# A two-layer mixer network in one program: every engine's order written out by hand, normalisation done in place

## Chip, core and metric

The kernel runs on one core of a Trainium2 chip. The metric is the device time of one execution in microseconds (us), the median of several runs. One more execution is taken by the hardware profiler; its times are those of the trace.

## What is computed

The input `x` is 256 rows of 1024 numbers; a vector `c` sets scale, shift and gate of each step (the modulation). Two layers follow, each a mixer and a feed-forward, with a layer norm after each of the four residual sums, then a hybrid mixer and a gated convolution. Cut to what matters:

```python
for i in range(DEPTH):                       # 2
    sh1, sc1, g1, sh2, sc2, g2 = split(silu(c) @ w_ada[i] + b_ada[i], 6)
    u = x * (1.0 + sc1) + sh1
    y = gla_mixer(u) if i == 0 else chunk_attention(u)
    x = layer_norm(ALPHA * x + (1 + g1) * y, ln_g, ln_b)
    u = x * (1.0 + sc2) + sh2
    y = square(relu(u @ w1)) @ w2            # 1024 -> 4096 -> 1024
    x = layer_norm(ALPHA * x + (1 + g2) * y, ln_g, ln_b)
x = x + hybrid_mixer(rms_norm(x))            # pooled, attention over chosen keys, gates
x = x + conv_ffn(rms_norm(x))
out = rms_norm(x)
```

All in float32. The GLA mixer is a gated linear attention in chunks of 64 rows, whose gate goes through a projection of 16 columns.

## The kernel before, in words

**Products.** A float32 product is made of three products in a shorter format (`mm3`, L264 to L268): each operand is a high part and a rest, and high x high, rest x high, high x rest are summed in PSUM. The weights come in chunks of at most 128x1024, in one list `CHUNKS` for the whole program. `load` (L247) fetches a chunk into a `raw` tile (four of these), ScalarE copies the high part (`hi`, L257), VectorE subtracts the rest (`lo`, L262). Near a phase's end the subtraction is made in two halves. Eight `hi`/`lo` pairs are held, and at times two more in the mixer's tiles `qk` and `v`. The same four `raw` tiles carry the weights of the modulation: `ada_gen` (L279) sums them on VectorE, L298 for the gates (into `acc`) and L300 for scale and shift.

**Rows.** The 256 rows are two halves `h` of 128. The mixers are a generator for each half, and `run` (L1273) lets half 0 go ahead by one chunk, at a phase's start and end by eight (`LEAD`), so that one half multiplies while the other is normalised. The feed-forwards take both halves together, with the last eight tiles half by half (`tail`).

**Startup** (L1168) makes scale and shift of the first step and multiplies the first 16 chunks (keys and values of the GLA mixer) into six PSUM banks: for each half two of the four `y` banks and one of the two `ps` banks. `gla_phase` empties them on ScalarE (L601 to L603) and then uses `ps` again for the projection to the first queries and the gate's 16 columns (`lr`, 272 wide); `lr` is copied by VectorE (L607), and `gla_core` transposes it and goes on.

**Layer norm.** `resid_ln` and `ln_chain`: VectorE adds gate times `y` to `x` into `z`, in two halves, with row statistics (L403 to L407); GpSimd makes rstd and shift in three steps (L410 to L412); ScalarE normalises both halves of `z` (L415); TensorE transposes `z` (L373), and `make_u` applies scale and shift and splits into `uh` and `ul`, the operands of the next phase. Gain and bias of the norm go into `x` afterwards (L393, L394).

**Order.** The startup is emitted in program order (`manual_schedule`). For all the rest a scheduler sorts the instructions of every engine: by the place where they were emitted, moved up by the offsets of `high_priority` blocks (`HPL`, `HPB`, `HPE`, ...), and by when it expects the operands. Each engine then runs its list in order; SyncE's list is that of the transfers.

Of the kernel before, what the change touches and what calls it, by code (L numbers as in the profile page):

```python
# [15 lines left out]
LN_EPS = 1e-5  # L16
# [7 lines left out]
HPL = 20  # L24
HPB = 234
HPE = 194
NACT = 5
XLOW = 40
FP = 88
W0 = 2  # L30
W1 = 8
HPC = 50
HPG = 0
# [5 lines left out]
F1 = 8  # L39
YL = 2  # L40
# [145 lines left out]
class K:  # L186
    def __init__(self, nc, tc, dr, out, dbg=None):
        self.nc, self.tc, self.dr, self.out, self.dbg = nc, tc, dr, out, dbg or {}
        self.loaded = 0
        self.ch = {}  # L190
        self.apos = self.bpos = 0
        self.uid = 0

    def nm(self, s):
        self.uid += 1
        return f"{s}_{self.uid}"

# [49 lines left out]
    def load(self):  # L247
# [22 lines left out]
    def split(self, src, n):  # L270

        xh = self.sb(512, f"hh{self.h}", 2, F32R)
        xl = self.sb(512, f"hl{self.h}", 2, F32R)
# [5 lines left out]
    def ada_gen(self):  # L279
# [3 lines left out]
        for idx, (layer, v) in enumerate(ADA):  # L283
# [23 lines left out]
            if gate:  # L307
# [3 lines left out]
                self.gate_rows(*late)  # L311
# [5 lines left out]
            yield  # L317

# [30 lines left out]
    def make_u(self, h, srcs, S, O):  # L349
        nc = self.nc  # L350
        uh, ul = (t[:, h * 1024:h * 1024 + 1024] for t in self.U)
        for j, src in enumerate(srcs):
            t = self.t2().rearrange("p (k t) -> p k t", t=128)
            sl = slice(j * 512, j * 512 + 512)
            if O is None and j == 1:
                nc.vector.tensor_tensor(t, src, S[:, j * 4:j * 4 + 4, None].to_broadcast([128, 4, 128]), op=ALU.mult)
            else:
                for k in range(4):
                    kk = j * 4 + k
                    if kk < NACT:  # L360
                        nc.scalar.activation(t[:, k, :], src[:, k, :], AF.Identity, scale=S[:, kk:kk + 1], bias=0.0 if O is None else O[:, kk:kk + 1])
                    else:
                        nc.vector.tensor_scalar(t[:, k, :], src[:, k, :], S[:, kk:kk + 1], O[:, kk:kk + 1], op0=ALU.mult, op1=ALU.add)
            t = t.rearrange("p k t -> p (k t)")
            nc.scalar.activation(uh[:, sl], t, AF.Copy)
            nc.vector.tensor_sub(ul[:, sl], t, uh[:, sl].bitcast(F32))
# [17 lines left out]
    def resid_ln(self, h, y, i, S, O):  # L384

        nc = self.nc
        x = self.x[h]
        with self.tc.high_priority(offset=HPL if h == 0 else HPB):
            pre = self.ln_chain(h, y, S, O)
        with self.tc.high_priority(offset=-XLOW):  # L390
            for j in range(2):
                sl = slice(j * 512, j * 512 + 512)
                nc.vector.tensor_mul(x[:, sl], pre[:, sl], self.lng[:, sl])  # L393
                nc.vector.tensor_add(x[:, sl], x[:, sl], self.lnb[:, sl])  # L394

    def ln_chain(self, h, y, S, O):
        nc = self.nc
        x = self.x[h]
        pre = self.sb(1024, "z")
        st = self.sb(12, "st", 2)  # L400
        for j in range(2):
            sl = slice(j * 512, j * 512 + 512)
            nc.vector.tensor_mul(pre[:, sl], y[j], self.Guse[:, sl])  # L403
            nc.vector.scalar_tensor_tensor(pre[:, sl], x[:, sl], ALPHA, pre[:, sl], op0=ALU.mult, op1=ALU.add)
            nc.vector.bn_stats(st[:, j * 6:j * 6 + 6], pre[:, sl])
# [7 lines left out]
        for j in range(2):  # L413
            sl = slice(j * 512, j * 512 + 512)
# [20 lines left out]
    def use(self, h):  # L435
        i = self.pos[h]
        self.pos[h] += 1
        if self.bg[h] is not None and next(self.bg[h], 0) == 0:
            self.bg[h] = None
# [122 lines left out]
    def ff_phase(self, after):  # L562
        nc = self.nc

        def squared(p):
            r = self.t2()
            with self.tc.high_priority(offset=HPE):
                nc.scalar.activation(r, p, AF.Relu)
            nc.scalar.activation(r, r, AF.Square)
            return r  # L570

        def head(h, tiles):
            for g in range(FFH // 4):
                yield from self.proj(h)
                self.h = h
                t = self.transposed(squared(self.res))
                self.keep_tiles(tiles, g * 4, self.split(t.rearrange("p k t -> p (k t)"), 512), 4, h)
                yield

        box = []  # L580

        def column(i, tiles):
# [4 lines left out]
            if i % 2 == 1:  # L587
                self.h = i // 2 % 2
                self.keep_tiles(tiles, i - 1, self.split(squared(p), 512), 2)
# [4 lines left out]
    def gla_phase(self, h, after):  # L594
# [17 lines left out]
        nc.scalar.activation(q[:, 256:], self.res, AF.Copy, scale=qs)  # L612
        yield
        pair = []
        for j in range(2):
            sl = slice(j * 512, j * 512 + 512)
            yield from self.proj(h)
            if j == 0:
                self.drain(h)
# [773 lines left out]
```

## Time and profile before

| | |
|---|---|
| median of 3 runs | 1071.26 us (1071.01 to 1071.87) |
| profiled execution | 1077.91 us |
| its span in the trace | 1076.1 us |
| granted TensorE clock, mean over the span | 0.987 |
| busy share of TensorE, VectorE, ScalarE, GpSimd | 95, 71, 53, 5% |
| moved by the transfers | 228.98 MB, 213 GB/s over the span |

The profiled execution is one of its own and 6.6 us above the median; every row of the trace belongs to it. TensorE's busy time is that of pipelined products, whose start to start time is shorter than one's duration. Granted clock is the share of full speed: 1.00 is 2.4 GHz, 0.50 is 1.2 GHz. "Idle before" of a row names what the engine waited for last.

### The profile page before, as it was taken

What the parts mean: (1) busy time and instruction counts of PE and PEld (TensorE: products, weight loads), DVE (VectorE), ACT (ScalarE), POOL (GpSimd) and SP (SyncE); (2) the same over time, 40 slices, a digit from 0 to 9 for tenths busy, and PEclk for the clock granted to TensorE, in tenths of its full rate; (3) what the DMA queues carried; (4) which work ended last, traced back from release to release, by engine and by line L of the source; (5) the groups of instructions that cost most, each with busy time, mean ns of one, the idle gap of its engine ahead of it and who ended that gap; (6) DMA issues with size and microseconds to landing.
All of it is one profiled execution on the core that took longest, in us unless ns stands there. A gap on an engine that the chain in (4) does not pass through costs nothing.

```text
span 1076.1 us, 15174 instructions
## 1 busy us (share of the span) xinstructions
PE 1025.8 (95%) x5628; PEld 856.0 (80%) x5628; DVE 759.3 (71%) x1162; ACT 572.8 (53%) x875; POOL 49.6 (5%) x93
## 2 busy tenths in 40 slices
PE   7999979999998999998999999899999999999997
PEld 4777757998986758686899888676878778999996
DVE  6879886777777776758666543788444678877764
ACT  4654456445555454535755553565555368655543
POOL 0000220000000000001000000200000001000000
PEclk9999999999999998999999999999999999999999
DMA  9998957888885685933877754344345655655521
GB/s 343 334 315 293 314 171 240 299 293 299 299 293 169 208 297 190 297 124 124 301 244 234 233 175 149 117 132 143 113 140 192 201 165 165 220 192 178 189 86 40
DMA packets 69478, 228.98 MB, mean 213 GB/s; under 512 B 7430, under 2 KB 12806, under 8 KB 69404
## 3 DMA queue, kind: packets, MB, share of 16 engines
q1 hardware_dynamic: 69404, 228.01, 62.9%
q8 instruction: 44, 0.72, 0.3%
q14 instruction: 30, 0.25, 0.1%
HBM read 226.93 MB, written 1.05 MB: 212 GB/s over the span
## 4 chain that ended last, share of the span: by engine, by line
PE 53%; DMA 13%; DVE 8%; ACT 6%; issue 3%; POOL 2%; POOLq 0%; ACTq 0%; SPq 0%; DVEq 0%
PE ps L266 10%; DMA raw<-in_w_dram 10%; PE ps L268 10%; PE ps L267 10%; PE y L266 6%; PE y L268 6%; PE y L267 6%; DMA raw<-in_ada_dram 3%; DVE lo L262 3%; ACT hi L257 3%; PE y L782 1%; PE pc L373 1%; PE y L756 1%; PE y L373 1%; DVE raw L300 1%
## 5 line engine op out<-in xcount | busy, mean ns | idle before, releaser
L262 DVE TENSOR_TENSOR lo<-raw,hi 128x1024 fp32r<-128x1024 f32 (+3 forms) x290 | 306.6, 1070 | 132.2 <-ACT hi L257 129.5
L257 ACT ACTIVATE hi<-raw 128x1024 fp32r<-128x1024 f32 (+2 forms) x250 | 262.5, 1055 | 256.1 <-DMA raw<-in_w_dram 84.1
L266 PE MATMUL ps<-hi,uh 128*128 128x512 f32 (+3 forms) x408 | 161.7, 396 | 2.1 <-ACT t L886 0.9
L267 PE MATMUL ps<-lo,uh 128*128 128x512 f32 (+3 forms) x408 | 159.1, 390 | 1.1 <-DVE lo L1260 1.1
L268 PE MATMUL ps<-hi,ul 128*128 128x512 f32 (+3 forms) x408 | 158.7, 389 | 0.0
L266 PE MATMUL y<-hi,hh 128*128 128x512 f32 x378 | 152.5, 403 | 3.7 <-ACT hh L274 3.7
L267 PE MATMUL ps<-ul,hi 128*128 128x256 f32 x536 | 151.3, 282 | 0.0
L268 PE MATMUL y<-hi,hl 128*128 128x512 f32 x378 | 151.0, 401 | 0.1
L266 PE MATMUL ps<-uh,hi 128*128 128x256 f32 x536 | 151.0, 282 | 0.0
L267 PE MATMUL y<-lo,hh 128*128 128x512 f32 x378 | 151.0, 399 | 0.0
L268 PE MATMUL ps<-uh,lo 128*128 128x256 f32 x536 | 150.8, 281 | 0.0
L266 PEld LDWEIGHTS ps<-uh,hi 128*128 128x128 f32 x536 | 100.8, 188 | 2.4
L267 PEld LDWEIGHTS ps<-ul,hi 128*128 128x128 f32 x536 | 100.5, 188 | 2.4
L268 PEld LDWEIGHTS ps<-uh,lo 128*128 128x128 f32 x536 | 101.3, 189 | 0.0
L266 PEld LDWEIGHTS ps<-hi,uh 128*128 128x128 f32 x408 | 78.2, 192 | 18.9 <-ACT t L886 1.6
L267 PEld LDWEIGHTS ps<-lo,uh 128*128 128x128 f32 x408 | 78.2, 192 | 17.3 <-DVE lo L1260 3.0
L268 PEld LDWEIGHTS ps<-hi,ul 128*128 128x128 f32 x408 | 77.9, 191 | 15.6 <-issue 1.6
L266 PEld LDWEIGHTS y<-hi,hh 128*128 128x128 f32 x378 | 71.9, 190 | 19.7 <-ACT hh L274 4.8
L268 PEld LDWEIGHTS y<-hi,hl 128*128 128x128 f32 x378 | 71.6, 190 | 18.2 <-DVE hl L275 1.5
L267 PEld LDWEIGHTS y<-lo,hh 128*128 128x128 f32 x378 | 71.8, 190 | 15.0 <-issue 0.7
L257 ACT ACTIVATE qk<-raw 128x1024 fp32r<-128x1024 f32 x42 | 44.5, 1061 | 50.5 <-DMA raw<-in_w_dram 20.7
L262 DVE TENSOR_TENSOR v<-raw,qk 128x1024 fp32r<-128x1024 f32 (+1 forms) x49 | 52.2, 1072 | 26.9 <-ACT qk L257 26.5
(290 smaller groups left out, 1526.0 us busy)
## 6 DMA issues: line engine op xcount, KB each, us to landing
raw<-in_w_dram SPq DMA_DIRECT2D x302, 512.0 KB, 4.3
raw<-in_ada_dram SPq DMA_DIRECT2D x80, 512.0 KB, 4.6
br<-in_rows_dram SPq DMA_DIRECT2D x12, 256.0 KB, 5.1
bias<-in_relb_dram SPq DMA_DIRECT2D x12, 256.0 KB, 5.8
lng<-in_rows_dram SPq DMA_DIRECT2D x5, 512.0 KB, 3.8
raw<-in_w_dram SPq DMA_DIRECT2D x8, 256.0 KB, 6.2
lnb<-in_rows_dram SPq DMA_DIRECT2D x4, 512.0 KB, 6.2
z<-in_ada_dram SPq DMA_DIRECT2D x3, 512.0 KB, 7.0
```

Of the source, the lines that this page charges most:

```text
L257: self.nc.scalar.activation(hi, raw, AF.Copy)
L262: self.nc.vector.tensor_sub(lo[:, sl], raw[:, sl], hi[:, sl].bitcast(F32))
L266: mm(out, xh, wh, start=start, stop=False)
L267: mm(out, xh, wl, start=False, stop=False)
L268: mm(out, xl, wh, start=False, stop=stop)
L300: nc.vector.scalar_tensor_tensor(raw, raw, 1.0, self.crow, op0=ALU.mult, op1=ALU.mult, accum_out=t[:, k:k + 1])
L373: self.nc.tensor.transpose(p[:, k * 128:k * 128 + 128], src[:, k * 128:k * 128 + 128], self.ident)
L756: nc.tensor.matmul(p[:, i * N:i * N + N], qT[r0:r0 + 64, hd // 2, :], kT[r0:r0 + 64, hd // 2, :N], start=True, stop=True)
L782: nc.tensor.matmul(o[:, hd * 64:hd * 64 + 64], pT[:, (i * nkb + kb) * 128:(i * nkb + kb) * 128 + 128], v[:, kb, hd * 64:hd * 64 + 64], sta ...
```

## The change

The scheduler is left out of the whole program: `run` is emitted under `manual_schedule`, so the order of emission is each engine's order. What should not stand at once behind its predecessor becomes a task. `mm3` counts time (0.000457 us per column for each of its three products at `self.clock`), and a task says with `yield` how much of that must be emitted before it goes on; `tick` runs the tasks that are due. Transposes, the GLA core, the attention cores and the last part of each normalisation are such tasks. The normalisation is done in place in `x` (ScalarE the first half, VectorE the second), and GpSimd keeps only the power. The halved subtraction is gone. The order of the transfers stays nearly the same.

```diff
     def mm3(self, out, xh, xl, wh, wl, start, stop):
...
+        self.clock += 3 * 0.000457 * out.free_size()
+        self.tick()
...
+    def spawn(self, gen):
+        task = [self.clock, gen]
+        self.tasks.append(task)
+        self.advance(task)
+        return task
+
+    def advance(self, task):
+        d = next(task[1], None)
...
+            task[0] = self.clock + d
+
+    def tick(self):
...
+        for task in list(self.tasks):
+            if task[1] is not None and task[0] <= self.clock:
+                self.advance(task)
...
-        n = raw.shape[1]
-        near = any(e - W0 <= self.loaded < e + W1 for e in ENDS[:-1])
-        for a in ((0, n // 2), (n // 2, n)) if near else ((0, n),):
-            sl = slice(*a)
-            self.nc.vector.tensor_sub(lo[:, sl], raw[:, sl], hi[:, sl].bitcast(F32))
+        self.nc.vector.tensor_sub(lo, raw, hi.bitcast(F32))
...
-            nc.vector.scalar_tensor_tensor(pre[:, sl], x[:, sl], ALPHA, pre[:, sl], op0=ALU.mult, op1=ALU.add)
-            nc.vector.bn_stats(st[:, j * 6:j * 6 + 6], pre[:, sl])
+            nc.vector.scalar_tensor_tensor(x[:, sl], x[:, sl], ALPHA, z[:, sl], op0=ALU.mult, op1=ALU.add)
+            nc.vector.bn_stats(st[:, j * 6:j * 6 + 6], x[:, sl])
         mv = self.sb(2, "mv", 2)
         nc.vector.bn_aggr(mv, st)
         v = self.sb(8, "rv", 4)
-        g = nc.gpsimd
-        g.tensor_scalar(v[:, 0:1], mv[:, 1:2], LN_EPS, None, op0=ALU.add)
-        g.tensor_tensor(v[:, 1:2], v[:, 0:1], self.mhalf[:, 0:1], op=ALU.pow)
-        g.tensor_scalar(v[:, 2:3], mv[:, 0:1], -1.0, v[:, 1:2], op0=ALU.mult, op1=ALU.mult)
-        for j in range(2):
-            sl = slice(j * 512, j * 512 + 512)
-            nc.scalar.activation(pre[:, sl], pre[:, sl], AF.Identity, scale=v[:, 1:2], bias=v[:, 2:3])
-        self.make_u(h, [self.transposed(pre[:, j * 512:j * 512 + 512]) for j in range(2)], S, O)
-        return pre
+        nc.vector.tensor_scalar(v[:, 0:1], mv[:, 1:2], LN_EPS, None, op0=ALU.add)
+        nc.gpsimd.tensor_tensor(v[:, 1:2], v[:, 0:1], self.mhalf[:, 0:1], op=ALU.pow)
+        nc.vector.tensor_scalar(v[:, 2:3], mv[:, 0:1], v[:, 1:2], -1.0, op0=ALU.mult, op1=ALU.mult)
+        nc.scalar.activation(x[:, sls[0]], x[:, sls[0]], AF.Identity, scale=v[:, 1:2], bias=v[:, 2:3])
+        nc.vector.tensor_scalar(x[:, sls[1]], x[:, sls[1]], v[:, 1:2], v[:, 2:3], op0=ALU.mult, op1=ALU.add)
+        yield 5.6
+        self.make_u(h, [self.transposed(x[:, sl]) for sl in sls], S, O)
+        if nxt is not None:
+            yield 12.0 if h == 0 else 8.0
+        for sl in sls:
+            nc.vector.tensor_mul(x[:, sl], x[:, sl], self.lng[:, sl])
+            nc.vector.tensor_add(x[:, sl], x[:, sl], self.lnb[:, sl])
...
-        nc.scalar.activation(q[:, :256], self.res[:, :256], AF.Copy, scale=qs)
         lr = self.sb(16, "lr", 2)
         nc.vector.tensor_copy(lr, self.res[:, 256:272])
+        nc.scalar.activation(q[:, :256], self.res[:, :256], AF.Copy, scale=qs)
         box = {}
-        self.bg[h] = self.gla_core(h, lr, q, k, v, box)
+        core = self.spawn(self.gla_core(h, lr, q, k, v, box))
...
     def gla_core(self, h, lr, q, k, v, box):

         nc = self.nc
+        yield 1.4
+        while h == 1 and "z" not in self.gla:
+            yield 0.7
         p = self.pc()
         nc.tensor.transpose(p[0:16, :128], lr, self.ident)
...
-        with self.tc.manual_schedule():
-            self.startup()
+        self.startup()
...
-            k.run()
+            with tc.manual_schedule():
+                k.run()
```

**ScalarE at the start of the GLA mixer.** `hi` are high parts of chunks 16 to 23, `v0`, `qk0`, `v1`, `qk1` the emptied startup banks; `ps_19` and `ps_22` are the two `ps` banks. Before:

```order
L257 ACTIVATE hi_104_458<-raw_103_456 128x816
L602 ACTIVATE qk0_131_536<-y_17_86 128x512
L257 ACTIVATE hi_107_464<-raw_106_462 128x816
L601 ACTIVATE v0_132_537<-ps_19_88 128x512
L603 ACTIVATE v0_132_537<-y_18_87 128x512
L602 ACTIVATE qk1_134_551<-y_20_89 128x512
L257 ACTIVATE hi_110_470<-raw_109_468 128x544
L601 ACTIVATE v1_135_552<-ps_22_91 128x512
```

And now (the five rows ahead of these are the `hi` of chunks 16 to 20):

```order
L279 ACTIVATE hi_120_509<-raw_119_507 128x1024
L279 ACTIVATE hi_123_515<-raw_122_513 128x1024
L279 ACTIVATE hi_126_521<-raw_125_519 128x1024
L631 ACTIVATE v0_132_536<-ps_19_88 128x512
L632 ACTIVATE qk0_131_535<-y_17_86 128x512
L633 ACTIVATE v0_132_536<-y_18_87 128x512
L631 ACTIVATE v1_135_551<-ps_22_91 128x512
L279 ACTIVATE hi_138_567<-raw_137_565 128x1024
```

The six copies moved behind all eight loads, and the first of them is the one from `ps_19`, whose bank the 272-wide projection `ps_133` uses next.

**VectorE at the same place.** `lo` are rests of chunks, `acc` the sum for the first gate over eight `raw` tiles, `lr` the gate's 16 columns. Before:

```order
L262 TENSOR_TENSOR lo_118_505<-raw_116_502,hi_117_504 128x1024
L607 COPY lr_151_625<-ps_133_541 128x16
L262 TENSOR_TENSOR lo_121_511<-raw_119_508,hi_120_510 128x1024
L607 COPY lr_152_634<-ps_136_556 128x16
L646 COPY glT_159_648<-pc_158_646 16x128
L262 TENSOR_TENSOR lo_124_517<-raw_122_514,hi_123_516 128x1024
```

And now:

```order
L280 TENSOR_TENSOR lo_127_522<-raw_125_519,hi_126_521 128x1024
L318 SCALAR_TENSOR_TENSOR acc_128_525<-raw_129_529,cact_14_83,acc_128_525 128x1024
...
L280 TENSOR_TENSOR lo_139_568<-raw_137_565,hi_138_567 128x1024
...
L280 TENSOR_TENSOR lo_145_601<-raw_143_598,hi_144_600 128x1024
L318 SCALAR_TENSOR_TENSOR acc_128_525<-raw_148_608,cact_14_83,acc_128_525 128x1024
L318 SCALAR_TENSOR_TENSOR acc_128_525<-raw_149_611,cact_14_83,acc_128_525 128x1024
L318 SCALAR_TENSOR_TENSOR acc_128_525<-raw_150_614,cact_14_83,acc_128_525 128x1024
L636 COPY lr_151_623<-ps_133_540 128x16
L636 COPY lr_152_632<-ps_136_555 128x16
```

The copy of `lr` stood behind `lo_118`; now three more `lo` (`lo_121`, `lo_124`, `lo_127`), two later ones and all eight sums stand ahead of it.

**ScalarE at the end of the first feed-forward.** `t2_618` is the last activation, `hh1_619` its high part. Before:

```order
L257 ACTIVATE hi_616_2952<-raw_615_2950 128x1024
L257 ACTIVATE hi_622_2990<-raw_621_2988 128x1024
L257 ACTIVATE qk1_625_3003<-raw_624_3001 128x1024
L257 ACTIVATE hi_628_3016<-raw_627_3014 128x1024
L568 ACTIVATE t2_618_2981<-ps_611_2906 128x512
L569 ACTIVATE t2_618_2981<-t2_618_2981 128x512
L274 ACTIVATE hh1_619_2984<-t2_618_2981 128x512
```

And now:

```order
L279 ACTIVATE hi_616_2943<-raw_615_2941 128x1024
L588 ACTIVATE t2_618_2971<-ps_611_2898 128x512
L589 ACTIVATE t2_618_2971<-t2_618_2971 128x512
L294 ACTIVATE hh1_619_2974<-t2_618_2971 128x512
L279 ACTIVATE hi_622_2980<-raw_621_2978 128x1024
L279 ACTIVATE qk1_625_2992<-raw_624_2990 128x1024
```

The activation moved ahead of three loads.

## Rows read from the trace of the kernel before

**Rows 1.** The page, busy us of each engine (share of the span):
```profile
PE 1025.8 (95%) x5628; PEld 856.0 (80%) x5628; DVE 759.3 (71%) x1162; ACT 572.8 (53%) x875; POOL 49.6 (5%) x93
```
**Rows 2.** Waits of TensorE: total us, times, longest
```profile
PE pc L373 <- ACT z L415: 17.8, 8, 4.1
...
PE y L266 <- ACT hh L274: 3.7, 1, 3.7
PE y L373 <- ACT cs L762: 2.6, 2, 1.8
...
PE pc L373 <- ACT t L569: 2.0, 2, 1.7
```
**Rows 3.** Windows: stretch, length, busy us by engine, granted clock, DMA share, GB/s
```profile
13.00:45.00 32.00, 31.12 (x127) 23.76 (x127) 30.24 (x60) 16.16 (x32) 0.99 (x2) 1.00 1.02 395
58.30:143.50 85.20, 78.85 (x382) 59.75 (x381) 75.75 (x119) 41.31 (x66) 12.31 (x14) 1.00 0.89 297
...
135.00:150.00 15.00, 11.22 (x46) 8.13 (x46) 10.92 (x25) 10.23 (x16) 4.68 (x5) 0.89 0.57 182
...
400.00:415.00 15.00, 15.00 (x67) 11.22 (x67) 8.61 (x13) 7.82 (x16) 0.20 (x1) 0.67 0.70 209
```
**Rows 4.** Timeline, third norm (after the first feed-forward): start, us, engine, line [idle before]
```profile
334.78 0.69 DVE L403 TENSOR_TENSOR z<-y,G 128x512 f32<-128x512 f32 x1 [1.15 <-PE y L268]
...
337.31 0.68 DVE L262 TENSOR_TENSOR lo<-raw,hi 128x512 fp32r<-128x512 f32 x1
...
337.90 0.20 DVE L407 BATCH_NORM_AGGREGATE mv<-st 128x2 f32<-128x12 f32 x1
...
338.20 0.55 POOL L410 TENSOR_SCALAR rv<-mv 128x1 f32<-128x1 f32 x1 [93.14 <-DVE mv L407]
...
338.83 0.99 POOL L411 TENSOR_TENSOR rv<-rv,mhalf 128x1 f32<-128x1 f32 x1
...
340.22 1.52 ACT L415 ACTIVATE z<-z,rv 128x512 f32<-128x512 f32 x2 [1.56 <-POOL rv L412]
...
341.09 0.44 PE L373 MATMUL pc<-const,z 128*128 128x128 f32 x2 [1.43 <-ACT z L415]
```
**Rows 5.** Timeline of VectorE at the start of the GLA mixer
```profile
58.06 0.17 DVE L607 COPY lr<-ps 128x16 f32<-128x16 f32 x1
...
62.45 1.20 DVE L262 TENSOR_TENSOR lo<-raw,hi 128x1024 fp32r<-128x1024 f32 x1
...
83.01 1.28 DVE L298 SCALAR_TENSOR_TENSOR acc<-raw,cact,acc 128x1024 f32<-128x1024 f32 x1
```
**Rows 6.** Timeline of TensorE at the same place
```profile
51.94 0.40 PE L268 MATMUL ps<-hi,ul 128*128 128x512 f32 x1
...
52.17 0.29 PE L266 MATMUL ps<-hi,uh 128*128 128x272 f32 x1
...
58.29 0.28 PE L643 MATMUL pc<-const,lr 128*16 128x128 f32 x1
```
**Rows 7.** Timeline of ScalarE and TensorE at the first feed-forward's end
```profile
321.07 1.06 ACT L257 ACTIVATE hi<-raw 128x1024 fp32r<-128x1024 f32 x1 [0.17 <-DMA raw<-in_w_dram]
...
326.98 1.06 ACT L257 ACTIVATE hi<-raw 128x1024 fp32r<-128x1024 f32 x1 [0.86 <-DMA raw<-in_w_dram]
...
327.95 0.58 ACT L568 ACTIVATE t<-ps 128x512 f32<-128x512 f32 x1
...
329.90 0.50 PE L266 MATMUL y<-hi,hh 128*128 128x512 f32 x1 [3.65 <-ACT hh L274]
```
**Rows 8.** Timeline of ScalarE at the start of the GLA mixer
```profile
50.26 0.60 ACT L601 ACTIVATE v<-ps 128x512 f32<-128x512 f32 x1
...
61.01 1.06 ACT L257 ACTIVATE hi<-raw 128x1024 fp32r<-128x1024 f32 x1 [0.81 <-DMA raw<-in_w_dram]
```
**Rows 9.** Timeline of VectorE in the attention
```profile
381.42 0.69 DVE L819 TENSOR_TENSOR cs<-y,bias 128x512 f32<-128x512 f32 x1
...
390.95 1.23 DVE L300 SCALAR_TENSOR_TENSOR raw<-raw,crow 128x1024 f32<-128x1024 f32 x1
```

More of the change, by code (lines that the diff above doesn't have):

```diff
@@ L39 @@
 F1 = 8
+NS = 8
 YL = 2
@@ L317, in ada_gen, with gate_last @@
             yield
+    def gate_last(self, *late):
+        yield 4.0
+        self.gate_rows(*late)
     def gate_rows(self, layer, v, acc):
@@ L566, in squared, with turn @@
             r = self.t2()
-            with self.tc.high_priority(offset=HPE):
-                nc.scalar.activation(r, p, AF.Relu)
+            nc.scalar.activation(r, p, AF.Relu)
             nc.scalar.activation(r, r, AF.Square)
             return r
+        def turn(h, g, tiles):
+            r = squared(self.res)
+            yield 2.4
+            t = self.transposed(r)
+            self.keep_tiles(tiles, g * 4, self.split(h, t.rearrange("p k t -> p (k t)"), 512), 4, h)
         def head(h, tiles):
@@ L587, in column @@
             if i % 2 == 1:
-                self.h = i // 2 % 2
-                self.keep_tiles(tiles, i - 1, self.split(squared(p), 512), 2)
+                self.spawn(kept(i, p, tiles))
             yield
@@ L612, in gla_phase, with gated @@
         nc.scalar.activation(q[:, 256:], self.res, AF.Copy, scale=qs)
+        box["q"] = True
         yield
         pair = []
+        tasks = []
+        def gated(j, sl, before):
+            while "o" not in box:
+                yield 0.7
+            self.finish(before)
+            if j == 0:
+                box["on"] = self.sb(1024, f"v{h}")
+                self.taken.add(h)
+            o, r, on = box["o"], box["r"], box["on"]
+            for d in range(2 * j, 2 * j + 2):
+                ds = slice(d * 256, d * 256 + 256)
+                nc.vector.scalar_tensor_tensor(on[:, ds], o[j][:, ds.start - j * 512:ds.stop - j * 512], r[:, d:d + 1], g2[:, ds], op0=ALU.mult, op1=ALU.mult)
+            yield 2.8
+            t = self.transposed(on[:, sl])
+            if j == 1:
+                self.taken.discard(h)
+            pair.append(self.split(h, t.rearrange("p k t -> p (k t)"), 512))
         for j in range(2):
@@ L742, in banks, with core @@
         return [[par + 2 * (b * nb + i) for i in range(nb)] for b in range(4 // nb) for par in range(2)]
-    def core_scores(self, h, qT, kT, pts, sums, score):
+    def core(self, h, g, qT, kT, pts, score, ready, box):
         nc = self.nc
@@ L749, in core_scores, with turn @@
         nb = 512 // N
+        nkb = h + 1
+        while not ready():
+            yield 0.7
+        sums = self.sb(8, "sums", 4)
+        groups = self.banks(nb)
+        def turn(s, pT):
+            t = self.transposed(s, bank=self.bank)
+            nc.scalar.activation(pT, t.rearrange("p k t -> p (k t)"), AF.Copy)
         last = None
-        for n, hs in enumerate(self.banks(nb)):
+        for n, hs in enumerate(groups):
             p = self.bank()
@@ L762, in core_scores @@
                 nc.scalar.activation(sv[:, i, :], sv[:, i, :], AF.Exp, bias=mx[:, i:i + 1], accum_out=sums[:, hs[i]:hs[i] + 1])
+            yield 2.8
             if last is not None:
-                self.core_turn(last, pts[n - 1])
+                turn(last, pts[n - 1])
             last = s
-            yield
-        self.core_turn(last, pts[n])
-    def core_turn(self, s, pT):
-        t = self.transposed(s, bank=self.bank)
-        self.nc.scalar.activation(pT, t.rearrange("p k t -> p (k t)"), AF.Copy)
-    def core_out(self, h, pts, sums, v, pair):
-        nc = self.nc
-        nkb = h + 1
-        nb = 4 // nkb
+        yield 1.4
+        turn(last, pts[n])
+        yield 1.4
+        while "v" not in box:
+            yield 0.7
+        v = box["v"]
         o = self.bank()
-        for hs, pT in zip(self.banks(nb), pts):
+        for hs, pT in zip(groups, pts):
             for i, hd in enumerate(hs):
@@ L1097, in rows_r @@
         nc = self.nc
+        dgs = []
+        for h in range(2):
+            dg = self.t2()[:, :128]
+            nc.vector.tensor_scalar(dg, self.ident, self.r[h], None, op0=ALU.mult)
+            dgs.append(dg)
+        yield 1.4
         p = self.pc()
@@ L1303, in room @@
             if self.loaded in SPARE:
-                return all(SPARE.get(i) != SPARE[self.loaded] for i in live)
+                pair = SPARE[self.loaded]
+                return pair not in self.taken and all(SPARE.get(i) != pair for i in live)
             return sum(i not in SPARE for i in live) < NB
```

484 lines of the change are left out of this document (250 added, 234 removed).

## Prediction

> **What bounds the kernel now.** The busy line comes first [rows 1]: TensorE works in 1025.8 of 1076.1 us. The change leaves its products as they are (the order of both kernels holds the same TensorE instructions, moved, with `x` for `z` as the operand of 64 transposes), so what can be won is its 50 us of idle time and what the half clock costs. The table of TensorE's waits says who ends the idle time [rows 2]: the largest entry, 17.8 us in 8 waits, is the transposes of the eight layer norms, which wait for ScalarE's `z`; then 3.7 us for one `hh`, 2.6 us for `cs`, 2.0 us for a `t` of the feed-forward. (Waits in the startup are left out: the change doesn't touch it.) Third, the stretches [rows 3]: four windows of 15 us (from 135, 320, 482 and 695 us, each with one of these waits in it; the first is shown) have a granted clock of 0.89, that is 0.11 x 15 = 1.65 us lost at 1.2 in place of 2.4 GHz, and one (400 to 415) has 0.67, a loss of 5 us. The DMA share is 0.89 from 58 to 143 us, with VectorE busy 75.75 of 85.2 us. So after the startup the kernel waits seldom, at known places, and early on VectorE and the transfers have little to spare. That makes the order on ScalarE and VectorE the thing to read: each runs its list in order, and whoever stands behind a load waits for that load's transfer.
>
> **The layer norms.** At 334.78 us VectorE takes the second bank of `y`, at 341.09 the first transpose starts, 1.43 us of which TensorE waited [rows 4]: a chain of 6.3 us. The change takes from it the half load ahead of the aggregate (0.6 us from its start to the aggregate's, since the loads now stand ahead of the chain) and two of GpSimd's three steps: 338.20 to 340.22 is 2.0 us, of which the power is 0.99; the two others go to VectorE, whose smallest copy takes 0.17 us [rows 5], so about 1.5 us. That leaves some 5.2 us. ScalarE normalises one half of 0.76 us as before, VectorE the other beside it. The cover, counted in the order, is now 24 products of 128x512 behind the last one on `y` (28 in the first norm, 43 narrow ones in the last) in place of 19 to 44. At 0.23 us each (51.94 to 52.17 [rows 6]) that is 5.6 us, 0.4 more than the chain. So the wait should go if nothing stands in front on either engine. If everything fits, all 17.8 us go; if one load of 1.2 us lies in the way each time, 8 x 0.8 = 6.4 stay. I leave half a microsecond each: **gain 13.8** (11.4 to 17.8). With the waits at 143, 488 and 697 us goes the half clock behind them: 3 x 1.65 = **5.0** (0 to 5.0).
>
> **The end of the first feed-forward.** TensorE waits 3.65 us until 329.90 for `hh`, since ScalarE ran the last `Relu` at 327.95, behind three more loads, the last of which waited for its transfer [rows 7]. In the new order it stands right behind the load that ran at 321.07. Relu, square and `hh` then end by about 325, before TensorE runs dry at 326.25: **gain 3.7 + 1.65 = 5.3** (0 if the bank is full only after 325). The same kind of move for `t` of L569: **gain 2.0** (0 to 2.0).
>
> **The start of the first mixer, first wait.** Here the new order is worse. Before, ScalarE empties the startup's banks between loads: `v<-ps` at 50.26 [rows 8], and the first 272-wide product, which needs that bank (there are two `ps`), follows at 52.17 without a gap [rows 6]. Now the same copy stands behind all eight loads from `hi_104_458` to `hi_126_521`. The last of these, at 61.01, waits for its transfer in the old trace too, and ends at 62.07; SyncE's list is the same up to there. With 0.60 us for the copy TensorE starts at 62.7: a **loss of 10.5**, sure to a microsecond. Behind it every product waits.
>
> **Second wait.** From the first 272-wide product to the transpose of `lr` are 6.1 us [rows 6]; with six products placed in between (0.7) and 1.65 for the clock after an idle stretch TensorE is there at 71.1. But the copy `lr<-ps`, at 58.06 before [rows 5], now stands on VectorE behind five loads and eight sums over `raw` for the modulation. Before, the last of these sums ran at 83.01 [rows 5], late partly because mixer work was mixed in. Without it the transfers set the pace: ten `raw` tiles of 128x1024 f32 (0.524 MB) and two rows of the norm follow the one that landed at 61.01, together 6.3 MB. At the 297 GB/s of 58 to 143 us that ends at 82.2, at the 395 of 13 to 45 us at 76.9 [rows 3]. I take 80, nearer to the stretch in question; with the sum (1.28) and the copy the transpose starts at 81.5, a wait of 10.4 us (7 to 13), and 1.65 for the clock after it.
> The Trainium skill (DMA: Bandwidth & Descriptors, Specifications) gives a limit of about 358 GB/s for one core's share of HBM and 435 for the fabric. The row of 395 GB/s already lies above the first; by an estimate with 435 the tiles land at 75.5, and the sum below would be some 4.5 us better.
>
> **What of it comes back.** At 81.5 TensorE stands where it stood at 58.29, less the 0.7: 22.5 us late, 24.1 with the clock. From 58.3 to 143.5 us it idled 85.2 - 78.85 = 6.35 us [rows 3], 3.4 of it the norm's wait, counted above. The other 3 us can be regained, since 16 us of loads and sums are then done ahead and VectorE is no longer short. **Loss 21** (17 with fast transfers, 26 with nothing regained).
>
> **The rest at nothing.** Loads near a phase's end are no longer split in halves on VectorE, the row sums and the copies of the hybrid mixer are spread out: VectorE is busy 71% [rows 1], TensorE's waits for these are 1 to 2 us, and a block of work there may be as late as before. If that cover is gone, each costs a microsecond or two. The attention I also put at nothing, see the third rival.
>
> **Sum.** -13.8 - 5.0 - 5.3 - 2.0 + 21 = -5.1 us against the profiled execution's 1077.9, that is 1072.8. That execution lies 6.6 above the median of the runs, 1071.3; the same step from the median gives **1066**. By the bounds of the terms the forecast could be 1058 to 1082.
>
> **Rivals.**
> 1. *The start costs less and the rest gives more.* The tiles land at the faster rate (loss 17), the norms lose all their wait, and the attention's 2.6 us and 5 us of half clock go too: -17.8 - 5 - 5.3 - 2 - 7.6 + 17 = -20.7, about 1050. For it: the same waits end in one way all over. Against it: the rate of 395 held only where no tile waited for a free buffer.
> 2. *Gain and loss cancel.* Mechanism as forecast, the norms regained to the lower bound and 24 at the start: about 1071, no change to be seen.
> 3. *Slower, by the attention.* Before, VectorE mixes the eight modulation sums with the score additions: the first addition ran at 381.42, the last sum at 390.95 [rows 9]. In the new order all eight stand ahead of the first addition, which then runs at about 392.1, 10.7 us later. Its exponentials and transposes follow, and TensorE reaches those after a count of 2.8 us of other products: up to 8 us of waiting, 1.65 for the clock. If more than the 5 us of net gain arrives here, the kernel is slower: -5 + 9.6 = +4.5, about 1076, and near 1084 with the norms at their lower bound and the start at 26. For it: the transfers set the pace of these sums there too (the window after it has a clock of 0.67). Against it: TensorE has the projections of both halves to run meanwhile, and the wait for `cs` was only 2.6 us.
>
> **How the numbers follow.** Forecast, 0.40; first rival 0.20; second 0.12; third 0.28. About 0.2%, 2 us, is what a measurement of this kernel tells from no change. Forecast and first rival are faster: 0.60; same 0.12; slower 0.28. The range for 8 in 10 goes from 1046, below the first rival, to 1086, above the third.
>
> **What would show it.** In the new profile the row of `v<-ps` should start near 62 and TensorE have a gap of 10 us until about 62.7, and a second of 7 to 13 us before the transpose of `lr`, near 81; the waits for `z` (now `x`) in the table should sum to about 4 us, the wait for `hh` at the end of the first feed-forward be gone, and the clock be full there. Wrong would be: the bank freed before 60 us, the copy of `lr` before 75, or norm waits still above 10 us. A wait of 5 us or more for `cs` would speak for the third rival.

## The result and the profile after

The changed kernel takes 1233.25 us (median of 4 runs, 1231.56 to 1234.93) against 1071.57 us of the kernel before in the same session: a ratio of 1.150 (95% interval 1.147 to 1.153), 162 us slower. Its profiled execution has a span of 1229.8 us, 153.7 more than before.

The page first: busy us of each engine, and the granted clock in 40 slices of 30.7 us.

```profile
PE 1063.9 (87%) x5628; PEld 893.3 (73%) x5628; DVE 782.8 (64%) x1149; ACT 561.8 (46%) x851; POOL 24.3 (2%) x77
...
PEclk9969998899999767989789999978899999899999
```

TensorE was idle 50.3 us before (1076.1 less the busy time of [rows 1]) and is idle 165.9 us now: 115.6 us. The other 38.1 us are the same products running longer, at 1.2 GHz: together the 153.7. So almost everything is waiting and what follows a wait.

The first transposes of the four norms (first half) mark off five stretches. They start at 143.50, 341.09, 486.87 and 678.99 us before, and at 171.35, 385.40, 579.30 and 792.93 us now:

| stretch | us before | us now | longer by |
|---|---|---|---|
| startup and first mixer | 143.5 | 171.4 | 27.9 |
| first feed-forward, with the end of the first norm | 197.6 | 214.1 | 16.5 |
| attention | 145.8 | 193.9 | 48.1 |
| second feed-forward | 192.1 | 213.6 | 21.5 |
| hybrid mixer, convolution, end | 397.1 | 436.8 | 39.7 |

Four windows tell more (stretch, length, busy us of PE, PEld, DVE, ACT and POOL, granted clock, DMA share, GB/s):

```profile
50.00:100.00 50.00, 25.29 (x130) 21.42 (x130) 29.54 (x32) 20.64 (x30) 0.45 (x2) 0.73 0.79 274
250.00:350.00 100.00, 100.00 (x632) 89.72 (x631) 71.91 (x84) 49.85 (x60) 0.99 (x2) 1.00 0.86 292
385.00:480.00 95.00, 63.20 (x245) 47.69 (x246) 53.69 (x78) 35.80 (x69) 1.95 (x7) 0.77 0.53 172
640.00:780.00 140.00, 140.00 (x881) 125.52 (x880) 74.32 (x69) 71.44 (x88) 0.00 (x0) 1.00 0.59 209
```

Inside the two feed-forwards (250 to 350, 640 to 780) nothing is lost at all. The loss lies at the start of each phase: the first mixer (50 to 100), the attention (385 to 480), and in the same way the feed-forwards' first 40 us and the hybrid mixer.

TensorE's waits after (total us, times, longest):

```profile
PE pc L398 <- ACT t L589: 24.3, 4, 9.3
PE pc L398 <- ACT x L428: 20.9, 5, 9.6
PE y L824 <- ACT qk L888: 17.6, 3, 15.7
PE ps L284 <- ACT qk L637: 13.3, 1, 13.3
PE pc L398 <- DVE ikw L1019: 12.9, 1, 12.9
PE pc L398 <- DVE t L882: 12.8, 4, 6.8
PE ps L284 <- ACT v L631: 10.0, 1, 10.0
...
PE y L284 <- ACT hh L294: 1.0, 1, 1.0
```

The norm's wait, 17.8 us in [rows 2], is 20.9 us (now `x`, not `z`); the wait for `hh` did go, 3.7 to 1.0 us; and six entries of 10 to 24 us are new or grown (`t` of the relu had 2.0 us in [rows 2], `t` of the attention 0.6). Four of the places follow.

**The start of the first mixer** (timeline, after; what answers to [rows 5, 6, 8]):

```profile
61.70 1.06 ACT L279 ACTIVATE hi<-raw 128x1024 fp32r<-128x1024 f32 x1 [0.96 <-DMA raw<-in_w_dram]
62.66 0.58 ACT L631 ACTIVATE v<-ps 128x512 f32<-128x512 f32 x1
```
```profile
63.29 0.60 PE L284 MATMUL ps<-hi,uh 128*128 128x272 f32 x1 [10.03 <-ACT v L631]
...
84.61 0.58 PE L284 MATMUL ps<-hi,uh 128*128 128x256 f32 x1 [13.28 <-ACT qk L637]
```
```profile
80.12 3.93 DVE L318 SCALAR_TENSOR_TENSOR acc<-raw,cact,acc 128x1024 f32<-128x1024 f32 x3 [2.87 <-DMA raw<-in_ada_dram]
83.97 0.25 DVE L636 COPY lr<-ps 128x16 f32<-128x16 f32 x2
```

The bank is emptied behind the eight loads, at 62.66; `lr` is copied behind the sums, at 83.97. The second wait stands six products earlier than forecast, at the bank that `lr` and the queries leave free, not at the transpose of `lr` (86.05).

**The start of the first feed-forward** (SyncE's queue, then ScalarE, VectorE's release and TensorE):

```profile
175.15 9.50 SPq L260 DMA_DIRECT2D raw<-in_w_dram  x5
210.51 0.33 SPq L447 DMA_DIRECT2D lng<-in_rows_dram  x1
211.24 0.33 SPq L448 DMA_DIRECT2D lnb<-in_rows_dram  x1
211.67 11.69 SPq L260 DMA_DIRECT2D raw<-in_w_dram  x6
```
```profile
209.80 0.69 DVE L435 TENSOR_TENSOR x<-x,lng 128x512 f32<-128x512 f32 x1
```
```profile
219.35 1.06 ACT L279 ACTIVATE hi<-raw 128x1024 fp32r<-128x1024 f32 x1 [10.68 <-DMA raw<-in_w_dram]
220.69 1.06 ACT L279 ACTIVATE hi<-raw 128x1024 fp32r<-128x1024 f32 x1 [0.28 <-DMA raw<-in_w_dram]
221.65 0.58 ACT L588 ACTIVATE t<-ps 128x512 f32<-128x512 f32 x1
```
```profile
222.94 1.12 PE L398 MATMUL pc<-const,t 128*128 128x128 f32 x4 [9.28 <-ACT t L589]
```

From 184.65 (175.15 + 9.50) to 210.51 SyncE starts no transfer. Its next one is `lng` for the coming norm, which may only overwrite the old row when the put-off gain step has read it, and that ends at 210.5. All weights stand behind it. The waits of SyncE's queue sum this up for the three norms:

```profile
SPq L447 <- DVE x L435: 60.7, 3, 25.8
```

Before, the same three waits were 8.9 us, the longest 4.0:

```profile
SPq L424 <- DVE x L393: 8.9, 3, 4.0
```

After this stop ScalarE waits 10.68 us for a weight, the relu behind that load waits too, and TensorE waits for the relu.

**The norm of the second half after the attention** (VectorE, then TensorE):

```profile
586.55 3.49 DVE L280 TENSOR_TENSOR lo<-raw,hi 128x1024 fp32r<-128x1024 f32 x3
591.33 1.23 DVE L280 TENSOR_TENSOR lo<-raw,hi 128x1024 fp32r<-128x1024 f32 x1 [1.29 <-ACT hi L279]
593.52 1.23 DVE L280 TENSOR_TENSOR v<-raw,qk 128x1024 fp32r<-128x1024 f32 x1 [0.97 <-ACT qk L279]
594.67 0.68 DVE L419 TENSOR_TENSOR z<-y,G 128x512 f32<-128x512 f32 x1
```
```profile
601.12 1.97 PE L398 MATMUL pc<-const,x 128*128 128x128 f32 x8 [9.57 <-ACT x L428]
```

The last product on this `y` started at 585.54. The chain begins 9 us later, behind loads two of which waited for transfers, and then takes 6.4 us (594.67 to 601.12).

**The attention's first score addition** (VectorE, then ScalarE):

```profile
453.12 1.23 DVE L320 SCALAR_TENSOR_TENSOR raw<-raw,crow 128x1024 f32<-128x1024 f32 x1 [1.44 <-DMA raw<-in_ada_dram]
...
455.67 0.69 DVE L877 TENSOR_TENSOR cs<-y,bias 128x512 f32<-128x512 f32 x1 [1.32 <-POOL bias L875]
```
```profile
457.12 0.40 ACT L830 ACTIVATE cs<-cs,mx 128x128 f32<-128x128 f32 x1 [14.65 <-DVE mx L828]
...
458.67 0.57 ACT L888 ACTIVATE qk<-pc 128x512 f32<-128x512 f32 x1
```

It runs behind the eight sums, and 1.3 us more pass until its bias is there. ScalarE's exponentials (L830) wait for it, behind these stands the copy of the next transposed keys (L888), and TensorE's next score products wait 15.7 us for that copy (`qk L888` in the table of waits).

### The profile page after: what moved, and what is told of

Read it like the earlier page. It is cut to its first block, busy times and chain, and to the rows that moved or that the text cites. A ratio compares the mean times of both kernels' runs of the same rounds, so it can differ in the third digit from the quotient of the medians.

```text
span 1229.8 us, 15186 instructions
## 1 busy us (share of the span) xinstructions
PE 1063.9 (87%) x5628; PEld 893.3 (73%) x5628; DVE 782.8 (64%) x1149; ACT 561.8 (46%) x851; POOL 24.3 (2%) x77
## 4 chain that ended last, share of the span: by engine, by line
PE 51%; DVE 16%; DMA 15%; ACT 10%; issue 7%; SPq 1%; POOL 0%; ACTq 0%; POOLq 0%; DVEq 0%
DMA raw<-in_w_dram 12%; PE ps L284 10%; PE ps L285 9%; PE ps L286 9%; PE y L286 5%; PE y L284 5%; PE y L285 5%; ACT hi L279 4%; DVE lo L280 4%; DMA raw<-in_ada_dram 2%; PE pc L398 2%; PE y L845 2%; ACT cs L830 1%; DVE raw L320 1%; PE y L824 1%
## 5 line engine op out<-in xcount | busy, mean ns | idle before, releaser
L280 DVE TENSOR_TENSOR lo<-raw,hi 128x1024 fp32r<-128x1024 f32 (+2 forms) x250 | 299.3, 1217 | 179.6 <-ACT hi L279 174.2
L279 ACT ACTIVATE hi<-raw 128x1024 fp32r<-128x1024 f32 (+2 forms) x250 | 255.6, 1046 | 167.1 <-DMA raw<-in_w_dram 100.2
L284 PE MATMUL ps<-hi,uh 128*128 128x512 f32 (+3 forms) x408 | 176.3, 432 | 28.0 <-ACT qk L637 13.3
L285 PE MATMUL ps<-lo,uh 128*128 128x512 f32 (+3 forms) x408 | 166.6, 408 | 1.0 <-DVE lo L1340 1.0
L286 PE MATMUL ps<-hi,ul 128*128 128x512 f32 (+3 forms) x408 | 165.3, 405 | 0.0
L284 PEld LDWEIGHTS ps<-hi,uh 128*128 128x128 f32 x408 | 86.1, 211 | 51.9 <-ACT qk L637 13.5
L285 PEld LDWEIGHTS ps<-lo,uh 128*128 128x128 f32 x408 | 86.1, 211 | 16.8 <-DVE lo L1340 2.6
L286 PEld LDWEIGHTS ps<-hi,ul 128*128 128x128 f32 x408 | 85.4, 209 | 17.6 <-DVE ul L391 0.5
L280 DVE TENSOR_TENSOR v<-raw,qk 128x1024 fp32r<-128x1024 f32 x42 | 51.3, 1221 | 25.7 <-ACT qk L279 24.3
L295 DVE TENSOR_TENSOR hl<-t,hh 128x512 fp32r<-128x512 f32 (+1 forms) x48 | 27.4, 570 | 58.9 <-ACT hh L294 58.9
```

Source lines behind the costliest of these rows:

```text
L279: self.nc.scalar.activation(hi, raw, AF.Copy)
L280: self.nc.vector.tensor_sub(lo, raw, hi.bitcast(F32))
L295: self.nc.vector.tensor_sub(xl[:, :n], src, xh[:, :n].bitcast(F32))
```

## The experiments

The theory after the comparison: not the tasks or the chain in `x` cost the time, but the fixed order, because at a phase's start each engine's list puts something urgent behind something that waits for a transfer or for another engine. The rival: the time is lost in one or two places only (the first mixer, SyncE's queue) and mending these gives it back. Differences below are taken between the ratios to the kernel before, times 1073 us; an interval of a ratio is 0.3 to 0.7% to either side, so a difference of two slow kernels is known to some 5 to 8 us.

**1. Order back to the scheduler.**

```diff
-            with tc.manual_schedule():
-                k.run()
+            k.run()
...
-        self.startup()
+        with self.tc.manual_schedule():
+            self.startup()
```

> The changed kernel, all but the startup handed back to the scheduler; the tasks, the counted amounts and the chain in x stay. If the fixed order itself costs the time, this runs near the kernel before: 1050 to 1090 us, with TensorE's idle time back near 50 us. If the tasks (transposes moved back behind other products, gain and bias of the norm put off) or the chain in x cost it, it stays above 1180 us.

Measured: 1068.3 us, ratio 0.993 (0.989 to 0.997). The same instructions, tasks and chain, sorted, are 0.7% faster than the kernel before. The waits of that run, from the largest:

```profile
PE ps L284 <- ACT uh L388: 6.9, 4, 2.6
...
PE pc L398 <- DVE t L882: 4.5, 3, 2.6
...
PE pc L398 <- ACT x L428: 1.2, 2, 0.8
```

So the whole loss is that of the fixed order; tasks and chain cost nothing where the scheduler sorts them. The norm's wait falls from 17.8 to 1.2 us. Part of it passes on to `uh`, which is made from the transposes: 6.9 us, where the kernel before has no such wait behind a norm.

**2. The norm's rows in another queue.**

```diff
-            self.nc.sync.dma_start(out=self.lng, in_=...)
-            self.nc.sync.dma_start(out=self.lnb, in_=...)
+            self.nc.gpsimd.dma_start(out=self.lng, in_=...)
+            self.nc.gpsimd.dma_start(out=self.lnb, in_=...)
```

> The changed kernel, gain and bias rows of the norms fetched by GpSimd's queue in place of SyncE's. Theory 1: in SyncE's list these two transfers wait for the put-off gain and bias of the norm before, and all weights behind them stand still (27 us without a weight transfer before 211.7 us). Then the three waits there shrink: 20 to 50 us faster than the changed kernel, 1185 to 1215 us. Theory 2: the waits come from the order on ScalarE and VectorE alone. Then it stays within 8 us of 1233 us.

Measured: 1211.3 us, ratio 1.129 (1.122 to 1.136): 23 us faster than the changed kernel. Between 184 and 211 us SyncE starts six weight transfers, where the changed kernel started one, and the wait for `t` of L589 falls from 24.3 to 9.1 us:

```profile
184.07 25.74 SPq L260 DMA_DIRECT2D raw<-in_w_dram  x6
```
```profile
PE pc L398 <- ACT t L589: 9.1, 4, 3.3
```

Theory 1 holds for this place, at the low end of what was expected.

**3. The start of the first mixer.**

```diff
+        # end of startup
+        for h in range(2):
...
+            nc.scalar.activation(v[:, 512:], acc[2], AF.Copy)
...
-        marks = [(15, 0), (F0, F1), (M0, 27), ...
+        marks = [(19, 0), (M0, 27), ...
...
-            while ... self.loaded < need + PF and room():
+            while ... self.loaded < need + (3 if self.pos[0] < 24 else PF) and room():
```

> The changed kernel, the six startup banks emptied right behind the startup's products, at most 3 chunks loaded ahead until chunk 24, and the sums for the gate begun only at chunk 19. If the start of the first mixer costs what the prediction's first and second wait said (10 and 13 us in the new trace, and two stretches at half clock worth some 10 us), it is 25 to 35 us faster than the changed kernel, about 1203 us. If the transfers set the end of this stretch anyway, under 10 us faster.

Measured: 1224.0 us, ratio 1.141 (1.134 to 1.148): 9 us faster, where the prediction's waits let 25 to 35 be expected; the second expectation, under 10 us, came true. In the window of 50 to 100 us TensorE is busy 39.22 instead of 25.29 us, so both waits did go. The half clock was worth less than the 10 us of the expectation: TensorE was busy for 3.9 and 3.0 us of the two stretches at 0.50 (56.9 to 67.2 and 74.0 to 87.6 us), half of which is 3.5. And the loads and sums that now come later are missed later:

```profile
97.00 1.06 ACT L279 ACTIVATE hi<-raw 128x1024 fp32r<-128x1024 f32 x1 [9.72 <-DMA raw<-in_w_dram]
```

TensorE has two new waits of 6 us each before the first norm. The rate of the transfers is not what sets this: it is 246 GB/s over 50 to 100 us, less than the 274 of the changed kernel. SyncE starts none from 86.75 to 92.73, until a subtraction that frees a `raw` tile has run:

```profile
81.37 5.38 SPq L316 DMA_DIRECT2D raw<-in_ada_dram  x3
92.73 6.94 SPq L260 DMA_DIRECT2D raw<-in_w_dram  x5
```
```profile
91.49 1.21 DVE L280 TENSOR_TENSOR lo<-raw,hi 128x1024 fp32r<-128x1024 f32 x1
```

Its operand was ready at 87.28 (the copy `hi` ran at 86.22), but eight instructions of the mixer stand ahead of it on VectorE. So the expectation came true for another reason than the one it gave: the transfers end this stretch, because the fixed order starts them late.

**4. The chain in x alone.** The kernel before, its scheduler kept, with the diff's chain in `ln_chain` (L419 to L429 of the change) in place of its own.

> The kernel before, still sorted by the scheduler, with the chain of the norm done in x alone: GpSimd's power only, one half normalised on ScalarE and one on VectorE. If the chain is a gain apart from the order, the eight waits (17.8 us) shrink to 6 to 14 us and the time to 1058 to 1069 us. If the scheduler's placing of the transposes sets the waits, it stays within 2 us of the kernel before.

Measured: 1064.2 us, ratio 0.992 (0.989 to 0.996), 0.8% faster than the kernel before; the norm's wait shrank further than expected, to a fifth of the 17.8 us of before:

```profile
PE pc L373 <- ACT x L412: 3.9, 2, 3.5
```

**5. The modulation sums spread in the attention.**

```diff
-        ..., (ENDS[1] + 7, 62), (ENDS[1] + 8, 63 + FINK), ...
+        ..., (ENDS[1] + 8, 63 + FINK), ...
```

> The changed kernel, the eight modulation sums that stand together ahead of the attention's first score addition spread over the twenty chunks before. If that block is what the addition waits for (the third rival's place; 15.7 us of TensorE waiting in the new trace and a long stretch at half clock), 15 to 25 us faster than the changed kernel, about 1213 us. If the addition is late for its bias rows, which SyncE fetches behind the same sums, or for the norm ahead, under 5 us faster.

Measured: 1230.1 us, ratio 1.144 (1.139 to 1.150): 6 us, no more than the intervals allow. The block did hold the addition: it now starts right behind the loads, and the wait of 15.7 us is 1.7. But the loads in front of it come 10 us later (439.02, the same two came at 429.06), and 8 of these are lost before the attention begins: the second norm's first transpose starts at 393.5 us (385.40 in the changed kernel), after a feed-forward of 223.0 us instead of 214.1. In its last 40 us (355 to 395) seven of the sums' transfers now stand among the weights, where two did; that they are what made it longer is argued, not tried.

```profile
439.02 2.52 DVE L280 TENSOR_TENSOR lo<-raw,hi 128x1024 fp32r<-128x1024 f32 x2 [7.91 <-ACT hi L279]
...
451.78 0.69 DVE L877 TENSOR_TENSOR cs<-y,bias 128x512 f32<-128x512 f32 x1 [0.21 <-issue]
```

The delay moved ahead by one phase.

**6. The attention's rows in the other queue too** (as 2, for `br` and `bias`).

> The run with the norm's rows on GpSimd's queue, with the attention's row transfers there too (its projection biases and score biases). If SyncE's list is held up in the attention as it was by the norm's rows (34 us of waiting for these in the new trace), 10 to 25 us faster than that run, about 1195 us. If the weights are early enough there, the same within 4 us: 1211 us.

Measured: 1214.7 us, ratio 1.130 (1.125 to 1.136), the same as run 2, as in the second expectation. Either nobody waits for what stands behind these transfers in SyncE's list, or GpSimd, whose list they now hold, takes the gain back; no run tells these apart.

**7. Edits 2, 3, 5 and 6 together.**

> The three edits together: startup banks emptied early and few loads ahead, norm's and attention's rows on GpSimd's queue, modulation sums spread. If they are separate places, the gains add: 9 + 22 to 40 + 15 to 25, about 1165 to 1185 us, and what is left above the kernel before is the order at the other phase starts (norm of the second half, first projections of the hybrid mixer). If one delay only uncovers the next, above 1195 us.

Measured: 1197.1 us, ratio 1.115 (1.108 to 1.121), 38 us faster than the changed kernel, the sum of the 23, 9 and 6 measured before, though each of these is known only to some 8 us. It lies above 1195 all the same, since runs 3 and 5 had gained less than their places cost. 123 us stay. So the rival falls: these places hold a quarter of the loss.

**8. The chain in x, and the square moved up with its relu** (kernel before with the chain of run 4; the line of `AF.Square` goes into the `high_priority` block).

> The kernel before with the chain in x (as in the fourth run), and the square of the feed-forward moved up with its relu. In the fourth run one wait for hh of 5.8 us at the end of the first feed-forward is left, where relu and square stand behind late loads. If the square was what stood back: 3 to 8 us faster than the fourth run, about 1058 us. If it is the relu's own place: the same, 1064 us.

Measured: 1064.1 us, ratio 0.990 (0.986 to 0.994), the same as run 4 within the intervals, as in the second expectation. The waits for `hh` fall from 7.2 us in run 4 to 4.3, the longest from 5.8 to 3.7, as in [rows 2]; that what is left is the relu's own place behind the loads is argued from the order. Runs 4 and 8 are the fastest of this study, and the first of them the simplest.

**9. Every counted amount half as long again.**

```diff
-            task[0] = self.clock + d
+            task[0] = self.clock + 1.5 * d
```

> The changed kernel, every counted amount half as long again, so that TensorE gets its transposes later behind other products and the two late steps of the norm are put off further. If the amounts are too short (TensorE runs into transposes whose chain is still on its way), 20 to 40 us faster than the changed kernel. If a chain's start is what is late, because other work stands ahead of it on VectorE and ScalarE, or the transfers, within 10 us of 1233 us, or slower by the gain and bias steps for which the next rows wait.

Measured: 1199.6 us, ratio 1.118 (1.112 to 1.124), 35 us faster by one number, as in the first expectation: the amounts were too short.

**10. Fewer loads ahead at a phase's end.**

```diff
-            while ... self.loaded < need + PF and room():
+            while ... self.loaded < need + (2 if any(e - 4 <= self.pos[1] < e for e in ENDS[:-1]) else PF) and room():
```

> The changed kernel, with at most two chunks loaded ahead during the last four chunks of a phase, so that fewer loads stand ahead of the second half's norm on VectorE (one in place of four after the attention). If loads ahead of the norm are what its transposes wait for (9.6 us after the attention, 20.9 us in all), that wait goes to about 3 us and the whole is 10 to 20 us faster. If the loads are then late for the next phase's first products, the wait changes its name and the time stays within 8 us of 1233 us.

Measured: 1237.9 us, ratio 1.154 (1.148 to 1.159), not faster. The norm's wait falls as expected, 20.9 to 6.2 us, and the relu's rises by 9.4:

```profile
PE pc L398 <- ACT t L589: 33.7, 4, 9.1
PE pc L398 <- DVE t L882: 17.8, 4, 8.1
...
PE pc L398 <- ACT x L428: 6.2, 4, 1.7
```

The loads ahead of the norm are what it waited for, and what the next phase needs. With a fixed list one of the two is late.

**11. Run 7 with the loads of run 10.**

> The three edits together with the held back loads. If the places add, 10 to 20 us below the run of the three edits, about 1182 us. If the delay moves on, 1190 to 1200 us.

Measured: 1197.0 us, ratio 1.116, as run 7: the delay moves on here too.

**12. The scheduled version with gain and bias not put off** (run 1, the `yield 12.0 if h == 0 else 8.0` left out).

> The changed kernel under the scheduler, with gain and bias of the norm no longer put off. If putting them off still holds back the next norm's rows and the transfers behind them in the sorted order, 3 to 10 us faster than the first run, about 1061 us; if the scheduler places them freely, the same 1068 us.

Measured: 1078.8 us, ratio 1.004 (1.001 to 1.007), 1.1% slower than run 1, which neither expectation had. The norm's wait is 5.9 us there, 1.2 in run 1. TensorE is idle for 50.4 us instead of 39.2. So under the scheduler putting the step off is a gain; under the fixed order run 2 shows what it costs through SyncE's list. No run leaves the delay out under the fixed order.

**13 to 15. Which amounts are too short.** 13 is run 7 with the amounts of run 9. In 14 only the norm's 5.6 us become 8.4; in 15 all amounts but the norm's three become half as long again.

> The three edits together and every counted amount half as long again. If the two are separate (36 and 34 us faster than the changed kernel), about 1163 us; if they mend the same waits, 1185 to 1200 us.

> The changed kernel, only the norm's transposes put further back: 8.4 us of counted products for 5.6. If the norm's cover is what the longer amounts mended (the chain takes 6.4 us in the new trace, 20.9 us of waits), 15 to 25 us faster than the changed kernel, about 1213 us, and the rest of the 34 us lies in the other tasks. If the norm's wait only passes on to the first products of the second half, within 6 us of 1233 us.

> The changed kernel, all counted amounts but the norm's (its 5.6 us, and the 12 and 8 us of gain and bias) half as long again. If the short amounts of 1.4 to 2.8 us behind each projection are what the longer ones mended (some 60 us of waits for t, ikw and qk in the new trace), 15 to 30 us faster than the changed kernel. If not, within 8 us of 1233 us.

Measured: 13: 1189.3 us, ratio 1.105 (1.100 to 1.110), 48 us faster than the changed kernel, where 38 and 35 would add to 73; so some 25 us are one and the same loss, mended in two ways. The feed-forwards of the table above show it: run 2 shortens the two by 9 and 11 us, run 9 by 11 and 11, run 13 by 7 and 11. And the first mixer takes 171.2 us in run 13, as in the changed kernel, where run 7 had 161.0. 14: 1227.0 us, ratio 1.142 (1.138 to 1.146), 8 us faster, between its two expectations. The wait for `x` goes, and part of it passes on to `uh`, which is made from it; the wait for `t` of L589 (24.3) goes too, and passes on to `hh`, which is made from `t`:

```profile
PE y L284 <- ACT hh L294: 16.4, 5, 7.5
PE ps L284 <- ACT uh L388: 12.3, 3, 6.8
```

15: 1209.0 us, ratio 1.126 (1.122 to 1.129), 26 us faster. So the amounts other than the norm's hold three quarters of what the longer amounts give, and the 8 us of run 14 are about the rest. The edit lengthens all of them (0.7 to 8.6 us), not only the 1.4 to 2.8 us behind each projection that the expectation names; which of them matter was not tried.

## Why the prediction was wrong

**Bounds of the kernel.** The three things it read hold: few waits at known places, the half clock behind them, little spare on VectorE and the transfers early on. The conclusion, that the order on ScalarE and VectorE is what to read, stopped one engine short: SyncE's list is one too.

**The start of the first mixer.** The two waits were right, nearly to the microsecond. First wait 10.5 forecast, 10.03 measured, TensorE starting at 63.3 (62.7). Second wait 10.4 (7 to 13), measured 13.3: the copy of `lr` at 83.97, where the forecast had the transpose behind it at 81.5. Between the waits the transfers ran at 315 GB/s, between the two rates of [rows 3] and below the 331 that landing at 80 asks for (6.3 MB from 61.01 on), and the last three sums ran in a row from 80.12, where the forecast had left one:

```profile
63.30:84.60 21.30, 8.03 (x48) 7.81 (x48) 13.52 (x13) 4.92 (x9) 0.00 (x0) 0.66 0.89 315
```

The figures of the Trainium skill (DMA: Bandwidth & Descriptors, Specifications), 358 and 435 GB/s, were not reached in this stretch, at these 315.

The net loss was not right. The first norm's transposes start 27.9 us late, where 21 and at most 26 were forecast: the 3 us "regained" were a guess with the wrong sign. And only 9 of these us came back in run 3.

**The end of the first feed-forward.** Right in the mechanism: the wait for `hh` went. The gain drowned in what follows. "The same kind of move for `t` of L569", a gain of 2.0, had the wrong sign: that wait is 24.3 us now (L589), and where it is longest, at the start of the first feed-forward, the relu stands behind a load that SyncE's list holds up.

**The norms: the step that failed first.** Forecast were 5.2 us of chain under 5.6 us of cover and 4 us of waits; measured 6.4 us and 20.9. Two terms were wrong. The chain was taken from [rows 4], where VectorE had done the first half of `y` before the second was ready; in the new order it comes late to both, and does six passes in a row (594.67 to 598.8). And "if nothing stands in front on either engine" was the condition on which everything hung: it was priced at half a microsecond each, and where it fails it costs 9 us after the attention (VectorE takes `y` at 594.67, the last product on it started at 585.54), because the loads in front wait for transfers themselves. Run 10 showed that: with fewer loads ahead the wait is 6.2 us. The chain itself is a gain, as said, but under the scheduler (runs 1 and 4).

**"The rest at nothing": the step that cost the prediction.** It does not name the delay of the norm's gain and bias at all, which puts it at nothing without a reason; of SyncE's list the prediction says only that it "is the same up to there". The list is nearly the same, but the moment at which its transfers may start is not: a transfer waits for the last reader of what it overwrites, and that reader was put off. Run 2 prices it at 23 us. The counted amounts of the other tasks are not priced either; what it says of late blocks of work is "each costs a microsecond or two". They hold 26 us (run 15).

**The third rival** had the sign and one of the places. Its price, 8 us of waiting at the first score addition, was 15.7 us. But the cause was not that block alone: without it (run 5) the time is nearly the same, since the loads ahead come 10 us later.

**The sum** was made place by place, each against a trace in which the neighbours were in time. That is what the fixed order takes away: a delay at one place holds the list of that engine, and through `raw` tiles and rows the transfers, and comes back at the next. Runs 3, 5, 10 and 14 all show a wait removed and another grown. The range, 1046 to 1086, was that of independent terms; the measured time lies far outside. (The bounds of the terms add to 1086 at the upper end, -11.4 + 26 on 1071.3, and not to the 1082 that stands there; this changes nothing.)

What stays open: 113 us remain in run 13 (its five stretches are 27.7, 9.1, 39.3, 10.2 and 27.0 us longer than before), and no run divides them among the lists of TensorE, VectorE and ScalarE. That all of it belongs to the order is shown by run 1; which engine's list it is was not tried apart.

## What to carry to other kernels

Before fixing an order by hand, ask at every urgent instruction what stands ahead of it on its engine and what that in turn waits for; if it is a transfer, the price is the transfer's delay and not the instruction's length, and part of it may have to be paid again at the next place, as in runs 3, 5, 10 and 14. A transfer waits for the last reader of what it overwrites, so putting off a reader puts off everything behind that transfer in its queue, even when the queue's list has not changed. And take a good part of a large change alone first: the chain in `x` under the old scheduler gave 0.8%, and the change that held it lost 15%.

## What was not expected of the hardware

How much the clock would add. The granted clock falls to 0.5 in most of the new waits and comes back late. In the first wait of the first mixer TensorE is idle from 53.3 to 63.29, and the clock is 0.50 from 56.9 to 67.2:

```profile
56.90:67.20 10.30, 3.91 (x17) 3.91 (x18) 7.90 (x7) 7.15 (x10) 0.00 (x0) 0.50 0.82 269
```

Until about 67 the 272-wide products start 0.23 us apart, then 0.13. Over 50 to 100 us the clock is 0.73, over 385 to 480 us 0.77, where the same window had 0.95 before. The same 5628 products are busy 38.1 us longer for it, a quarter of the whole loss. The forecast had 1.65 us for each wait; for the two waits of the first mixer that was about right (half of the 3.9 and 3.0 us that TensorE was busy in them), but there are some twenty such stretches now, and were five before.
